# Pair sums of the seven-product chains written back into PSUM, gate products and gated additions on VectorE

## The chip, the core and the metric

The kernel runs on one core of one Trainium2 chip. A core has five engines that matter here: TensorE (PE; its weight loads are shown as PEld), VectorE (DVE), ScalarE (ACT), GpSimd (POOL) and SyncE (SP), which issues the DMAs. Each has its own queue and runs it in order; they wait for each other through semaphores. Matmul results land in PSUM (eight banks), everything else lives in SBUF. The metric is the device time of one execution, in microseconds (us).

## What is computed

One layer of a diffusion backbone for two token groups: 128 context and 512 latent tokens, 640 columns in the kernel, which keeps channels on the partitions. Shapes are D_MODEL = 1024, D_FF = 2816, all float32. The change touches the two SwiGLU feed-forward steps (up and down projection) and the projection of the GLA branch.

```python
def swiglu(h, w_gate, w_up, w_down):
    return (jax.nn.silu(h @ w_gate) * (h @ w_up)) @ w_down

def trunk_layer(x, mod, ...):
    h = modulate(rms_norm(x, norm_ffn1), sh1, sc1)
    x = x + 0.5 * gt1 * swiglu(h, w_ffn1_gate, w_ffn1_up, w_ffn1_down)
    h = modulate(rms_norm(x, norm_mix), sh2, sc2)
    y = mixer(h, ...)      # ends: y = (g_a * branch_a + g_b * (o @ w_proj_gla)) @ w_out
    x = x + gt2 * y
    h = modulate(rms_norm(x, norm_ffn2), sh3, sc3)
    return x + 0.5 * gt3 * swiglu(h, w_ffn2_gate, w_ffn2_up, w_ffn2_down)
```

## The kernel before

**Products.** A float32 matmul is made of three passes on a high and a low part of each operand. `split` (L108, L109) makes them: ScalarE copies the high part, VectorE subtracts it for the low part. Both weights and activations are split in this way.

**Seven products in place of eight.** A job (`Pair7`) is a 2 x 2 block product: two output tiles of 128 rows (i = 0, 1), each of two halves of NH = 320 columns. It is computed by the seven-product scheme. Four sums of weight blocks, S1 to S4 (L492, L494, L496, L498), are made by GpSimd in the raw weight tile, each needed by later splits of that tile. `prep` runs the list STEPS up to a wanted step. For a gate or up job a product is 4 x 3 = 12 matmuls of 128 x 320 (L516), for a down job 9 or 6.

**Strides and banks.** `Pipe.stride` runs one job, with the tail of the job before it (`prev`) and the first weight steps of the job after it (`ahead`) put in between. A job takes three PSUM banks of six that turn: A for products 1, 6, 7 and 4, C for product 2, B for products 5 and 3. TensorE's order in a stride is 1, 2, then 3 of the job before (tail3), 6, 5, then 4 of the job before (tail4), 7.

**Take hooks.** After each product a hook takes what it needs. In the class `Take`, `p1`, `p16` and `p167` copy bank A to SBUF on ScalarE (u, w, u: L605 or L657, L613, L617), because A goes on accumulating; `p2`, `p5` and `p53` add a pair on VectorE (u + C, u + B, w + B); `p1674` takes the finished A. The third product is added onto B, so TensorE waits there until p5 has read B (L620 for a gate job, L664 for others); the seventh is added onto A, so TensorE waits until p16 has copied A (L613).

**The jobs the change touches** use `TakeMul`, where a pair sum does not go out but is put onto a tile `into`: p2, p5 and p53 add in SBUF (L664), and `onto` multiplies on GpSimd (L661) for an up job (`into` is the SiLU of the gate) and for the last projection (`TakeY`, `into` is the branch gate read from DRAM). `TakeDown.onto` (L774) adds gate times sum to the residual stream X on VectorE. After p53 of an up job `Hidden7.first` subtracts the halves of x0 (L707, GpSimd), and place 1 of the next stride splits x0 into high and low; `second` does the same for x1 with three more sums (L719 to L721). The last part of each feed-forward step uses `HiddenPlain`, without sums.

**Order.** Each feed-forward step runs a list of jobs: gate, the four down jobs of the part before, up, then gate, up, gate, up. There are 20 up jobs, 24 down jobs and four `TakeY` jobs in all. In the feed-forward steps `pin` fixes every engine's order to the order in which the code is written; the last projection is not pinned, and there a scheduler places instructions. Weight loads are issued by SyncE when a raw tile comes free.

## Time and profile before

| | |
|---|---|
| median of 3 runs | 1566.56 us (1566.31 to 1567.09) |
| the profiled execution | 1564.67 us, span 1562.9 us |
| TensorE busy | 1481.5 us, 95% of the span |
| VectorE busy | 1175.6 us, 75% |
| ScalarE busy | 785.7 us, 50% |
| GpSimd busy | 582.2 us, 37% |
| waits of TensorE in L516 | 42.2 us |
| granted TensorE clock, mean | 0.989 |

The span is the time from the first to the last instruction; a busy share is an average over stages. In the rows below an instruction is named by its line, engine, operation and tiles (out<-in, buffer numbers left out): wraw is a raw weight tile, wspl a split weight, pb a PSUM bank, g the tiles x0, x1 and `into`, hn and sqh the copies u and w, pg a page of activations.

### The profile page before, as it was taken

Reading aid. Unit: us, or ns where it says so; the run is one execution under the profiler, and the core shown is the slowest. Engines: PE = TensorE matmul, PEld = TensorE weight load, DVE = VectorE, ACT = ScalarE, POOL = GpSimd, SP = SyncE. Lnnn points to the kernel's source line nnn. Section 1 sums busy time; section 2 is a strip of 40 time slices with the busy share of each in tenths; the row PEclk is TensorE's granted clock in tenths of the full one; section 3 lists DMA queues with packets and bytes.
Section 4 is the critical chain, followed back from the end, with each engine's and each line's share of the span. In section 5 each row is a group of like instructions: output and inputs, shape, how many; then the busy total and the mean of one; then the engine's idle time right before and its main releaser. Section 6 shows DMA issues by size and latency. Waiting matters only on the chain.

```text
span 1562.9 us, 27799 instructions
## 1 busy us (share of the span) xinstructions
PE 1481.5 (95%) x10994; PEld 1429.8 (91%) x10994; DVE 1175.6 (75%) x2001; ACT 785.7 (50%) x1687; POOL 582.2 (37%) x470
## 2 busy tenths in 40 slices
PE   7989999999999999999899999999999998998997
PEld 6988889999998999999899998999898998998997
DVE  6759769769768688385866658778777967977976
ACT  5535445445555546454454445346545445544554
POOL 1534655564620000001234314620355565566440
PEclk8999999999999999999999999999999999999999
DMA  9454222222235320222148456354211321321232
GB/s 361 146 211 141 81 68 95 82 68 95 82 102 190 110 68 32 90 65 89 56 172 279 168 182 237 124 192 148 82 55 62 102 82 44 112 71 59 96 103 100
DMA packets 150426, 183.54 MB, mean 117 GB/s; under 512 B 4799, under 2 KB 124983, under 8 KB 150295
## 3 DMA queue, kind: packets, MB, share of 16 engines
q1 hardware_dynamic: 150295, 181.76, 34.8%
q8 instruction: 86, 1.41, 0.4%
q14 instruction: 45, 0.37, 0.1%
HBM read 167.59 MB, written 14.16 MB: 116 GB/s over the span
## 4 chain that ended last, share of the span: by engine, by line
PE 47%; DVE 30%; POOL 10%; ACT 5%; issue 5%; DMA 2%; POOLq 0%; SPq 0%; ACTq 0%; DVEq 0%
PE pb L516 16%; DVE wspl L109 13%; PE pb L139 6%; PE pb L386 5%; PE mm L1040 5%; DVE pg L774 5%; DVE pg L109 4%; POOL g L661 3%; ACT wspl L108 3%; PE mm L139 2%; POOL wraw L496 2%; PE sc L1189 2%; DVE hn L664 2%; POOL wraw L498 2%; PE sm L215 2%
## 5 line engine op out<-in xcount | busy, mean ns | idle before, releaser
L516 PE MATMUL pb<-pg,wspl 128*128 128x320 f32 x5556 | 839.7, 311 | 42.2 <-DVE g L620 15.1
L516 PEld LDWEIGHTS pb<-pg,wspl 128*128 128x128 f32 x5556 | 819.7, 189 | 59.4 <-DVE g L620 19.3
L109 DVE TENSOR_TENSOR wspl<-wraw,wspl 128x512 fp32r<-128x512 f32 (+2 forms) x676 | 513.3, 780 | 197.2 <-ACT wspl L108 195.3
L108 ACT ACTIVATE wspl<-wraw 128x512 fp32r<-128x512 f32 (+2 forms) x676 | 378.8, 588 | 254.2 <-POOL wraw L496 74.5
L496 POOL TENSOR_TENSOR wraw<-wraw 128x512 f32<-128x512 f32 (+2 forms) x74 | 89.8, 1214 | 241.2 <-DVE wspl L109 227.7
L494 POOL TENSOR_TENSOR wraw<-wraw 128x512 f32<-128x512 f32 (+2 forms) x74 | 104.1, 1407 | 102.0 <-DVE wspl L109 102.0
L386 PE MATMUL pb<-pg,wspl 128*128 128x320 f32 (+2 forms) x864 | 132.7, 311 | 1.6 <-DVE wspl L109 1.6
L386 PEld LDWEIGHTS pb<-pg,wspl 128*128 128x128 f32 x864 | 127.2, 188 | 2.1 <-DVE wspl L109 1.9
L498 POOL TENSOR_TENSOR wraw<-wraw 128x512 f32<-128x512 f32 (+2 forms) x74 | 110.0, 1486 | 3.1
L139 PE MATMUL pb<-pg,wspl 128*128 128x320 f32 x672 | 105.2, 315 | 3.0 <-DVE pg L1460 2.7
L139 PEld LDWEIGHTS pb<-pg,wspl 128*128 128x128 f32 x672 | 100.5, 190 | 5.1 <-DVE pg L1460 4.0
L492 POOL TENSOR_TENSOR wraw<-wraw 128x512 f32<-128x512 f32 (+2 forms) x74 | 96.4, 1303 | 4.2
L109 DVE TENSOR_TENSOR pg<-g,pg 128x640 fp32r<-128x640 f32 x86 | 85.1, 1006 | 16.0 <-ACT pg L108 16.0
L108 ACT ACTIVATE pg<-g 128x640 fp32r<-128x640 f32 x86 | 58.4, 682 | 63.8 <-DVE g L679 26.0
L1040 PE MATMUL mm<-wspl,pg 128*128 128x256 f32 x672 | 88.9, 289 | 0.1
L1040 PEld LDWEIGHTS mm<-wspl,pg 128*128 128x128 f32 x672 | 83.9, 195 | 0.5 <-ACT pg L1142 0.3
L1243 POOL TENSOR_TENSOR rs<-ms,negh 128x5 f32<-128x5 f32 x4 | 4.7, 1175 | 208.1 <-DVE ms L1241 208.1
L661 POOL TENSOR_TENSOR g<-g,hn 128x320 f32<-128x320 f32 x48 | 53.2, 1109 | 62.8 <-DVE hn L664 51.3
L109 DVE TENSOR_TENSOR pg<-pg,pg 128x320 fp32r<-128x320 f32 (+2 forms) x84 | 57.3, 729 | 11.9 <-ACT pg L108 11.7
L613 ACT ACTIVATE sqh<-pb 128x320 f32<-128x320 f32 x74 | 31.8, 430 | 54.1 <-PE pb L516 54.1
L617 ACT ACTIVATE hn<-pb 128x320 f32<-128x320 f32 x74 | 31.8, 430 | 41.4 <-PE pb L516 41.4
L131 PE MATMUL pb<-pg,wspl 128*128 128x320 f32 x288 | 48.0, 321 | 3.9 <-DVE pg L366 1.9
(219 smaller groups left out, 1745.6 us busy)
## 6 DMA issues: line engine op xcount, KB each, us to landing
pg<-in_w_ada_dram SPq DMA_DIRECT2D x72, 512.0 KB, 7.0
wraw<-in_w_ffn_gate_dram SPq DMA_DIRECT2D x22, 1024.0 KB, 5.0
wraw<-in_w_ffn_up_dram SPq DMA_DIRECT2D x22, 1024.0 KB, 5.0
wraw<-in_w_ffn_down_dram SPq DMA_DIRECT2D x28, 768.0 KB, 4.4
wraw<-in_w_in_dram SPq DMA_DIRECT2D x22, 512.0 KB, 3.5
wraw<-in_w_in_dram SPq DMA_DIRECT2D x10, 1024.0 KB, 5.5
wraw<-in_w_out_dram SPq DMA_DIRECT2D x8, 1024.0 KB, 5.2
wraw<-in_w_ffn_down_dram SPq DMA_DIRECT2D x12, 512.0 KB, 3.4
```

Of the source, the lines that this page charges most:

```text
L108: S.activation(out=hi, in_=src, func=AF.Copy)
L109: eng.tensor_tensor(out=lo, in0=src, in1=hi.bitcast(F32), op=ALU.subtract)
L139: T.matmul(out=bank(ps, hf)[:, 0:NH], lhsT=w[a][k], rhs=acts[k][:, b, hf * NH:(hf + 1) * NH], start=(k == 0 and ti == 0), stop=(k == nk - ...
L386: T.matmul(out=ps[:, 0:c1 - c0], lhsT=w[a][i], rhs=acts[i][:, b, c0:c1], start=(i == 0 and ti == 0), stop=(i == nk - 1 and ti == 2))
L492: G.tensor_tensor(out=self.a21, in0=self.a21, in1=self.a22, op=ALU.add)
L494: G.tensor_tensor(out=self.a11, in0=self.a22, in1=self.a11, op=ALU.subtract)
L496: G.tensor_tensor(out=self.a11, in0=self.a11, in1=self.a21, op=ALU.subtract)
L498: G.tensor_tensor(out=self.a12, in0=self.a12, in1=self.a11, op=ALU.subtract)
L516: T.matmul(out=bank, lhsT=self.w[i][s][k], rhs=x[k][:, t, :], start=first and k == 0 and ti == 0, stop=k == self.n - 1 and ti == 2, skip_g ...
L661: return G.tensor_tensor(out=x, in0=x, in1=part, op=ALU.mult)
L774: V.scalar_tensor_tensor(out=self.X[k][:, a:b], in0=x[:, o:o + b - a], scalar=self.gate[:, k, r:r + 1], in1=self.X[k][:, a:b], op0=ALU.mul ...
L1040: T.matmul(out=ps_out, lhsT=h2[k][:, a, t * P:(t + 1) * P], rhs=w[b][k], start=(k == 0 and ti == 0), stop=(k == KD - 1 and ti == 2))
```

## The change

The sum of p2, p5 and p53 is written into a PSUM bank instead of SBUF: p2 into C, p5 into C again (`self.free`), p53 into B. The bank is then an operand of what follows. The gate products of `onto` move from GpSimd to VectorE, with one operand in PSUM. The gated addition of the down jobs reads the sum from PSUM. `Hidden7.first` does product and difference on VectorE, the product in PSUM; where it is called without a bank (the first pair of each feed-forward step) the difference moves to VectorE too. In p16 ScalarE's copy of A is now written ahead of the product.

```diff
@@ -652,36 +652,30 @@
     class TakeMul(Take):
 
 
-        def p1(self, ps):
-            self.u = sm_tile([P, NH], "hn")
-            S.activation(out=self.u, in_=ps, func=AF.Copy)
-
-        def onto(self, part, i, hf):
+
+        def p2(self, ps):
+            V.tensor_tensor(out=ps, in0=self.u, in1=ps, op=ALU.add)
+            self.free = ps
+
+        def p16(self, ps):
+            Take.p16(self, ps)
+            self.onto(self.free, 0, 0)
+
+        def onto(self, ps, i, hf):
             x = self.into[i][:, hf * NH:(hf + 1) * NH]
-            return G.tensor_tensor(out=x, in0=x, in1=part, op=ALU.mult)
-
-        def add(self, part, ps):
-            V.tensor_tensor(out=part, in0=part, in1=ps, op=ALU.add)
-
-        def p2(self, ps):
-            self.add(self.u, ps)
-
-        def p16(self, ps):
-            self.onto(self.u, 0, 0)
-            Take.p16(self, ps)
+            V.tensor_tensor(out=x, in0=ps, in1=x, op=ALU.mult)
 
         def p5(self, ps):
-            self.add(self.u, ps)
-            self.mixed = self.onto(self.u, 1, 1)
+            V.tensor_tensor(out=self.free, in0=self.u, in1=ps, op=ALU.add)
+            self.onto(self.free, 1, 1)
 
         def p1674(self, ps):
-            x = self.into[1][:, 0:NH]
-            V.tensor_tensor(out=x, in0=ps, in1=x, op=ALU.mult)
+            self.onto(ps, 1, 0)
             self.done(1)
 
         def p53(self, ps):
-            self.add(self.w, ps)
-            self.last = self.onto(self.w, 0, 1)
+            V.tensor_tensor(out=ps, in0=self.w, in1=ps, op=ALU.add)
+            self.onto(ps, 0, 1)
             self.done(0)
 
     class Hidden7:
@@ -697,14 +691,19 @@
             split(h[:, 0, :], h[:, 1, :], x)
             return h
 
-        def first(self, x0):
+        def first(self, x0, ps=None):
             def work():
                 h = self.put(x0)
                 self.b11.append(even(h))
                 self.t1.append(odd(h))
 
             self.x0 = x0
-            G.tensor_tensor(out=x0[:, NH:N], in0=x0[:, NH:N], in1=x0[:, 0:NH], op=ALU.subtract)
+            right = x0[:, NH:N]
+            if ps is None:
+                V.tensor_tensor(out=right, in0=right, in1=x0[:, 0:NH], op=ALU.subtract)
+            else:
+                V.tensor_tensor(out=ps, in0=ps, in1=right, op=ALU.mult)
+                V.tensor_tensor(out=right, in0=ps, in1=x0[:, 0:NH], op=ALU.subtract)
             pipe.at(1, work)
 
         def second(self, x1):
@@ -746,7 +745,8 @@
 
             pipe.at(place, work)
 
-        def first(self, x):
+        def first(self, x, ps):
+            V.tensor_tensor(out=x[:, NH:N], in0=ps, in1=x[:, NH:N], op=ALU.mult)
             self.put(x, 1)
 
         def second(self, x):
@@ -760,22 +760,23 @@
             self.into = self.g.x0, self.g.x1
             TakeMul.p1(self, ps)
 
+        def p53(self, ps):
+            V.tensor_tensor(out=ps, in0=self.w, in1=ps, op=ALU.add)
+            self.hid.first(self.into[0], ps)
+
         def done(self, i):
-            (self.hid.second if i else self.hid.first)(self.into[i])
+            self.hid.second(self.into[i])
 
     class TakeDown(TakeMul):
         def __init__(self, mp, gate, X):
             self.mp, self.gate, self.X = mp, gate, X
 
-        def onto(self, x, i, hf):
+        def onto(self, ps, i, hf):
             k = 2 * self.mp + i
             for r, a, b in HSEG[hf]:
                 o = a - hf * NH
-                V.scalar_tensor_tensor(out=self.X[k][:, a:b], in0=x[:, o:o + b - a], scalar=self.gate[:, k, r:r + 1],
+                V.scalar_tensor_tensor(out=self.X[k][:, a:b], in0=ps[:, o:o + b - a], scalar=self.gate[:, k, r:r + 1],
                                        in1=self.X[k][:, a:b], op0=ALU.mult, op1=ALU.add)
-
-        def p1674(self, ps):
-            self.onto(ps, 1, 0)
 
         def done(self, i):
             pass
```

How the order moves is shown at three places. The first two are the same stretch of the first feed-forward step: the end of the up job of f = 10 (blocks 10 and 11 of D_FF; its `into` tiles are g_2594 and g_2595) and the gate job of f = 12 behind it (raw weights wraw_3065), while the weights of the next up job (wraw_3179) are prepared. GpSimd's queue before, from S2 of the gate job (L494):

```order
L494 TENSOR_TENSOR wraw_3065<-wraw_3065 128x4x128
L661 TENSOR_TENSOR g_2595<-g_2595,hn_3258 128x320
L498 TENSOR_TENSOR wraw_3065<-wraw_3065 128x4x128
L661 TENSOR_TENSOR g_2594<-g_2594,sqh_3213 128x320
L707 TENSOR_TENSOR g_2594<-g_2594 128x320
L496 TENSOR_TENSOR wraw_3179<-wraw_3179 128x4x128
L492 TENSOR_TENSOR wraw_3179<-wraw_3179 128x4x128
L494 TENSOR_TENSOR wraw_3179<-wraw_3179 128x4x128
```

and with the change:

```order
L494 TENSOR_TENSOR wraw_3065<-wraw_3065 128x4x128
L498 TENSOR_TENSOR wraw_3065<-wraw_3065 128x4x128
L496 TENSOR_TENSOR wraw_3179<-wraw_3179 128x4x128
L492 TENSOR_TENSOR wraw_3179<-wraw_3179 128x4x128
L494 TENSOR_TENSOR wraw_3179<-wraw_3179 128x4x128
L720 TENSOR_TENSOR g_2594<-g_2595,g_2594 128x320
L498 TENSOR_TENSOR wraw_3179<-wraw_3179 128x4x128
```

The three instructions of `onto` and `first` are gone; S4 (L498) follows S2 at once, and S3 of the next job (L496) follows S4; L720 there is L721 before. VectorE's queue over the same stretch, from p5's sum to p1674; before:

```order
L664 TENSOR_TENSOR hn_3258<-hn_3258,pb_3219 128x320
L109 TENSOR_TENSOR wspl_3262<-wraw_3065,wspl_3262 128x512
L109 TENSOR_TENSOR wspl_3282<-wraw_3065,wspl_3282 128x512
L609 TENSOR_TENSOR g_3297<-hn_3280,pb_3267 128x320
L109 TENSOR_TENSOR wspl_3300<-wraw_3065,wspl_3300 128x512
L109 TENSOR_TENSOR wspl_3305<-wraw_3179,wspl_3305 128x512
L664 TENSOR_TENSOR sqh_3213<-sqh_3213,pb_3219 128x320
L109 TENSOR_TENSOR wspl_3323<-wraw_3179,wspl_3323 128x512
L109 TENSOR_TENSOR wspl_3341<-wraw_3179,wspl_3341 128x512
L109 TENSOR_TENSOR pg_3359<-g_2594,pg_3359 128x640
L679 TENSOR_TENSOR g_2595<-pb_3144,g_2595 128x320
```

and with the change, from p5's sum on:

```order
L669 TENSOR_TENSOR pb_3145<-hn_3258,pb_3219 128x320
L666 TENSOR_TENSOR g_2595<-pb_3145,g_2595 128x320
L109 TENSOR_TENSOR wspl_3262<-wraw_3065,wspl_3262 128x512
L109 TENSOR_TENSOR wspl_3282<-wraw_3065,wspl_3282 128x512
L609 TENSOR_TENSOR g_3297<-hn_3280,pb_3267 128x320
L109 TENSOR_TENSOR wspl_3300<-wraw_3065,wspl_3300 128x512
L109 TENSOR_TENSOR wspl_3305<-wraw_3179,wspl_3305 128x512
L764 TENSOR_TENSOR pb_3219<-sqh_3212,pb_3219 128x320
L705 TENSOR_TENSOR pb_3219<-pb_3219,g_2594 128x320
L706 TENSOR_TENSOR g_2594<-pb_3219,g_2594 128x320
L109 TENSOR_TENSOR wspl_3323<-wraw_3179,wspl_3323 128x512
L109 TENSOR_TENSOR wspl_3341<-wraw_3179,wspl_3341 128x512
```

Behind p5's sum stands its product (L666), and behind p53's sum (L764) product and difference (L705, L706), ahead of the weight split that followed the sum before. The third place is the last projection, where the scheduler orders VectorE's work: the first strides' p2 and p53 (g_10668 and g_10790 are the `into` tiles of the first and the second job). VectorE before:

```order
L664 TENSOR_TENSOR hn_10796<-hn_10796,pb_10777 128x320
L109 TENSOR_TENSOR wspl_10836<-wraw_10711,wspl_10836 128x512
L664 TENSOR_TENSOR sqh_10733<-sqh_10733,pb_10739 128x320
L109 TENSOR_TENSOR wspl_10855<-wraw_10711,wspl_10855 128x512
L1488 TENSOR_TENSOR g_10668<-g_10668,pg_10255 128x640
L109 TENSOR_TENSOR pg_10670<-g_10668,pg_10670 128x640
```

and with the change:

```order
L657 TENSOR_TENSOR pb_10777<-hn_10796,pb_10777 128x320
L666 TENSOR_TENSOR g_10790<-pb_10777,g_10790 128x320
L109 TENSOR_TENSOR wspl_10836<-wraw_10711,wspl_10836 128x512
L677 TENSOR_TENSOR pb_10739<-sqh_10732,pb_10739 128x320
L666 TENSOR_TENSOR g_10668<-pb_10739,g_10668 128x320
L109 TENSOR_TENSOR wspl_10855<-wraw_10711,wspl_10855 128x512
L1489 TENSOR_TENSOR g_10668<-g_10668,pg_10255 128x640
L109 TENSOR_TENSOR wspl_10889<-wraw_10711,wspl_10889 128x512
L109 TENSOR_TENSOR pg_10670<-g_10668,pg_10670 128x640
```

The product of p16 of the second job (g_10790) stands right behind its p2, the product of p53 of the first (L666 onto g_10668) between p53's sum and the addition L1489, which is L1488 before.

## Rows read from the trace of the kernel before

**Rows 1.** The page, parts 1 and 4: busy us (share) xinstructions; the chain's shares.

```profile
PE 1481.5 (95%) x10994; PEld 1429.8 (91%) x10994; DVE 1175.6 (75%) x2001; ACT 785.7 (50%) x1687; POOL 582.2 (37%) x470
...
PE 47%; DVE 30%; POOL 10%; ACT 5%; issue 5%; DMA 2%; POOLq 0%; SPq 0%; ACTq 0%; DVEq 0%
```

**Rows 2.** Waits of TensorE: us in total, times, longest us.

```profile
PE pb L516 <- DVE g L620: 15.1, 15, 3.5
PE pb L516 <- ACT sqh L613: 12.4, 14, 1.2
PE pb L516 <- DVE hn L664: 6.7, 5, 2.8
PE pb L516 <- DVE pg L109: 6.0, 11, 0.9
```

**Rows 3.** Windows: stretch, us, then busy us (x) of PE, PEld, DVE, ACT, POOL.

```profile
298.00:326.10 28.10, 25.37 (x169) 24.64 (x168) 20.69 (x28) 13.82 (x29) 17.38 (x13) 1.00 0.24 76
...
361.50:418.00 56.50, 56.50 (x385) 56.50 (x386) 51.60 (x81) 29.80 (x61) 31.71 (x26) 1.00 0.30 98
```

**Rows 4.** Timeline of the pair: start us, us, instruction xcount [idle before <-releaser].

```profile
283.98 1.27 POOL L661 TENSOR_TENSOR g<-g,hn 128x320 f32<-128x320 f32 x1 [1.03 <-DVE hn L664]
...
285.20 1.75 POOL L498 TENSOR_TENSOR wraw<-wraw 128x512 f32<-128x512 f32 x1
...
288.86 0.48 DVE L664 TENSOR_TENSOR sqh<-sqh,pb 128x320 f32<-128x320 f32 x1
...
290.76 0.88 POOL L707 TENSOR_TENSOR g<-g 128x320 f32<-128x320 f32 x1
291.60 1.30 POOL L496 TENSOR_TENSOR wraw<-wraw 128x512 f32<-128x512 f32 x1
292.93 0.63 ACT L108 ACTIVATE wspl<-wraw 128x512 fp32r<-128x512 f32 x1 [3.21 <-POOL wraw L496]
...
298.11 0.48 DVE L620 TENSOR_TENSOR g<-hn,pb 128x320 f32<-128x320 f32 x1
...
298.64 7.47 PE L516 MATMUL pb<-pg,wspl 128*128 128x320 f32 x48 [0.60 <-DVE g L620]
...
305.16 0.48 DVE L642 TENSOR_TENSOR g<-sqh,pb 128x320 f32<-128x320 f32 x1
...
306.84 0.42 ACT L613 ACTIVATE sqh<-pb 128x320 f32<-128x320 f32 x1
...
307.31 12.87 PE L516 MATMUL pb<-pg,wspl 128*128 128x320 f32 x86 [1.20 <-ACT sqh L613]
...
326.71 7.46 PE L516 MATMUL pb<-pg,wspl 128*128 128x320 f32 x48 [1.54 <-DVE g L620]
```

**Rows 5.** Groups by line: busy us, mean ns | idle; L720 by itself: ns min/median/max.

```profile
L661 POOL TENSOR_TENSOR g<-g,hn 128x320 f32<-128x320 f32 x48 | 53.2, 1109 | 62.8 <-DVE hn L664 51.3 <-ACT g L643 10.4 <-issue 1.1
...
L707 POOL TENSOR_TENSOR g<-g 128x320 f32<-128x320 f32 x17 | 15.5, 910 | 1.2
...
L664 DVE TENSOR_TENSOR sqh<-sqh,pb 128x320 f32<-128x320 f32 x48 | 22.9, 478 | 2.8 <-PE pb L516 2.8
...
L720 DVE TENSOR_TENSOR g<-g x17: 491/492/1054, 102.4 to 1441.8; 128x320 f32<-128x320 f32 x17
...
L774 DVE SCALAR_TENSOR_TENSOR pg<-sqh,hg,pg 128x128 f32<-128x128 f32 x24 | 26.9, 1120 | 0.0
...
L393 DVE SCALAR_TENSOR_TENSOR pg<-pb,hg,pg 128x128 f32<-128x128 f32 x24 | 7.6, 344 | 1.8 <-PE pb L386 1.8
```

**Rows 6.** Last projection and second feed-forward step: timeline; a window, PEclk third last.

```profile
999.86 1.91 DVE L1488 TENSOR_TENSOR g<-g,pg 128x640 f32<-128x640 f32 x1 [1.61 <-POOL g L661]
...
1023.53 10.54 PE L516 MATMUL pb<-pg,wspl 128*128 128x320 f32 x60 [2.79 <-DVE hn L664]
...
1174.45 7.78 PE L516 MATMUL pb<-pg,wspl 128*128 128x320 f32 x33 [3.54 <-DVE g L620]
...
1174.50:1180.40 5.90, 5.90 (x22) 5.90 (x23) 5.87 (x9) 2.87 (x5) 2.80 (x2) 0.50 0.00 0
```

## The prediction, made before the change was run

> **What bounds the kernel now.** The page first: TensorE is busy for 95% of the span and VectorE for 75%, and the chain that ended last runs 47% through TensorE, 30% through VectorE and 10% through GpSimd [rows 1]. So a change that takes no matmul away can only give back what TensorE idles, and the next view is TensorE's waits. In the seven-product chains (L516) four waits carry nearly all of it: 15.1 us for L620, 12.4 for L613, 6.7 for L664 and 6.0 for the hidden splits of L109 [rows 2]. All four are evictions or splits on VectorE or ScalarE, yet the engine behind them is not full. In the stretch of four down jobs TensorE does 385 matmuls in 56.50 us without a stall (0.147 us each); in a pair of one up and one gate job it is busy for 25.37 of 28.10 us and VectorE for 20.69 [rows 3]. A pair is 2 x 7 x 12 = 168 matmuls, 24.7 us at that pace. From the first third-product restart to the next one (298.64 to 326.71, 28.07 us) 3.4 us are lost, 1.20 + 1.54 of them as the two gaps shown [rows 4]. The other 0.65 is the restart: 0.3 us for each stall.
>
> The timeline of one such pair says why [rows 4]. At 283.98 GpSimd multiplies the p5 half of the up job (L661); step S4 of the weights (L498) stands behind it and starts at 285.20, and the weight splits that wait for S4 hold VectorE until p53's sum at 288.86. Then GpSimd multiplies again, subtracts (L707, 290.76) and only then does S3 of the next job (L496, 291.60). ScalarE, which needs S3 for the next weight split, sat idle for 3.21 us, until 292.93. From there the delay runs through VectorE to L620 at 298.11: the pair sum of the gate job, which reads bank B before TensorE may add its third product there. TensorE waits 0.60 us, in the next pair 1.54. From L620 to L642 VectorE has work in its queue without a pause of note; L642 at 305.16 lets ScalarE do its SiLU and then L613 (306.84), and TensorE's seventh product waits 1.20 us for that.
>
> **The change part by part.** *Taken from GpSimd:* the 72 gate products of L661 (three in each of 24 jobs: the 48 of the row and 24 like them) at 1.11 us and the 17 differences of L707 at 0.91 [rows 5]: 95 us of GpSimd. What counts is not the sum but the places: S4 no longer stands behind a product that waits for p5, nor S3 behind two that wait for p53.
>
> *Given to VectorE:* 89 instructions of 320 columns with one operand in PSUM. The sum of this kind from PSUM takes 0.478 us [rows 5]: 42.5 us in all, 1.9 us for an up job that feeds a Hidden7 (15 of them), 1.4 for the other nine jobs, and two differences by themselves. Writing the sum into PSUM stands in no row. Not below 0.48, since the same columns go through; the upper bound is the slowest 320-column row of two operands, 1.05 [rows 5]. I take 0.48: reading PSUM made these sums no slower than the best case of two SBUF operands (0.49).
>
> *Made cheaper on VectorE:* the gated additions of the 24 down jobs now read PSUM. From SBUF the 128-column piece took 1.12 us, from PSUM in another stage 0.34 [rows 5]: 0.78 for that piece alone, so some 19 us over 24 jobs, and the 192-column piece beside it gains too. This lies in stretches where TensorE does not wait [rows 3]; I count nothing for it. If that cover went, it would only be a gain.
>
> *In the pair*, hand-walked on the trace's clock. TensorE stops at 298.64 - 0.60 = 298.04, after the second product of the next up job. Counted back by 0.147 us a matmul the gate job began at 282.2, the third product in its stride ended at 287.5, its sixth at 289.2, its fourth (in the tail) at 292.8, its seventh at 294.5. S4 can start some 2 us sooner, so VectorE is free at 287.5 and p53's three instructions end at about 289, where L707 ended at 291.6. S3 is done long before; the next weight split follows L613 at about 289.7, not 292.93. Then the hidden split, the fourth product's eviction (292.8), the second split and the copy of the seventh product (294.6) bring L620 to about 295.7 to 296.2, against 298.04, when TensorE needs it: a margin near 2 us in place of a stall of 0.6 or 1.5. L642 follows L620 by 7.05 us and L613 follows by 1.68 more [rows 4]; by the earlier L620 L613 starts at 304.4 and ends at 304.9. The seventh product is due at 298.04 + 48 x 0.147 = 305.1. That margin is thin, and the up job now has one more VectorE product (0.48) ahead of the seventh weights' split, and another behind p5. What is queued behind these: the split's low half, and on GpSimd S2, which waits for it; GpSimd's own product no longer stands ahead of S1, which pays for that. So I count the L620 waits as gone and half of the L613 waits.
>
> *The banks:* C is now held to p5 and B through the product. Six banks turn, three for each job, so C's bank is wanted again two jobs later, some 10 us after its last reader. This costs nothing; the cover is the rotation, and with it gone TensorE would wait for p5 once a job. The orders of TensorE and of the DMA queue are as before; ScalarE's differs only in the last projection.
>
> *The last projection.* There x0's addition (L1488) waits 1.61 us for GpSimd and then runs 1.91 us beside GpSimd's S2 [rows 6]. The products are now on VectorE ahead of it. It starts some 2 us sooner, and the waits for L664 of this stage, the longest of them 2.79 us, come from its lateness, by way of the hidden split and p5 behind it on VectorE. That stall and the one of 3.54 us in the second FFN were each followed by slow matmuls, in the second case at a granted clock of 0.50, the lower level of 1.2 GHz: 60 matmuls took 10.54 us and 33 took 7.78, where 0.147 each gives 8.8 and 4.9 [rows 6]. Without the 0.2 us that a last matmul runs on, 4.3 us go with the two stalls.
>
> *The sum:* L620 15.1 + 15 x 0.3 = 19.6; L613, half, 6.2 + 7 x 0.3 = 8.3; L664, four fifths, 5.4 + 4 x 0.3 = 6.6; hidden splits, two thirds (the first down job's t2 split has little slack), 4.0 + 7 x 0.3 = 6.1; clock 4.3. Together 44.9 us. The profiled execution took 1564.67 us, 1.8 of them outside its span of 1562.9, and the median of the runs is 1.9 above it: 1564.7 - 44.9 + 1.9 = **1521.7 us**. The ceiling is all four waits: 40.2 + 45 x 0.3 + 4.3 = 58 us, 1508.6.
>
> **The rivals.** *A: only the first stall goes.* L642 and L613 stand in VectorE's and ScalarE's own queues, and the new products there eat what is gained. For it: 7 us of VectorE work between L620 and L642. Against it: that work starts from L620, which comes sooner. Then only L620 and its clock loss (2.7) go: 22.3 us, 1544.3.
>
> *B: slower, VectorE becomes the bound in the pairs.* The up job's four added instructions make 20.69 + 1.9 = 22.6 us of VectorE in a pair that TensorE needs 24.7 for. It turns once the four instructions of a pair that write PSUM cost 0.5 us more, over 1.0 each, which is the far end above. If then every added instruction lies on the path, 42.5 us: 1609. Against it: no row from PSUM is anywhere near 1.0. The Trainium skill has a rule that points this way (Perfetto Trace Analysis, Optimizing Scalar/DVE Operations): with VectorE saturated, work may be handed to GpSimd; this change does the reverse. By that rule the price would be the same 42.5 us, but its condition, a saturated VectorE, is not what the pairs show.
>
> *C: no change.* The steps S1 to S4, still 1.3 to 1.75 us each, collide with VectorE's splits wherever they now fall, and the sooner start is used up before L620: 1566.6. Against it: ScalarE's 3.21 us of idle time ends with S3, which has nothing left to stand behind.
>
> **How the numbers follow.** The forecast 0.69 (by itself 1508 to 1533), A 0.20, B 0.06, C 0.05. The range runs from the ceiling past A: 1508 to 1547. Faster by over 0.2%, about what a measurement of this kernel can tell from no change: 0.89; within it 0.05; slower 0.06.
>
> **What would show it.** Right: L620 gone from TensorE's waits or under 2 us, L613 between 3 and 8, S3 starting within 0.5 us of its weights, a pair period near 25 us, no lower clock in the last projection and the second FFN, VectorE's total within 15 us of 1176. Wrong: PSUM-written sums well over 0.5 us; VectorE without idle time in the pairs; waits of the same size under other names, above all for a weight split that waits for GpSimd's S2.

## The result, and the profile after

The changed kernel takes **1515.36 us** (median of 4 runs, 1514.91 to 1516.08); the kernel before, in 4 runs beside it, 1566.43 us (1564.15 to 1567.09). The ratio is 0.9677, 95% interval 0.966 to 0.9694: 51 us less. The profiled execution took 1515.8 us, its span is 1514.0.

The page of the changed kernel, parts 1 and 4, answers to [rows 1]:

```profile
PE 1466.2 (97%) x10994; PEld 1424.7 (94%) x10994; DVE 1160.6 (77%) x2090; ACT 783.5 (52%) x1687; POOL 492.1 (33%) x381
...
PE 76%; DVE 13%; issue 3%; ACT 3%; DMA 3%; SPq 1%; POOL 1%; ACTq 0%; POOLq 0%; DVEq 0%
```

VectorE has 89 instructions more and yet 15.0 us less of busy time; GpSimd has 90 us less. TensorE's share of the last chain went from 47 to 76%.

TensorE's waits in the seven-product chains of the changed kernel (us in total, times, longest us), against [rows 2]:

```profile
PE pb L516 <- ACT sqh L613: 2.8, 7, 1.2
...
PE pb L516 <- DVE pb L669: 1.8, 4, 0.7
...
PE pb L516 <- DVE g L620: 1.5, 1, 1.5
...
PE pb L516 <- DVE wspl L109: 0.4, 1, 0.4
```

L669 is p5's sum, L664 before. The waits of L516 went from 42.2 to 6.4 us. The pair of [rows 4], up f = 10 and gate f = 12, looks like this in the timeline of the changed kernel (start us, us, instruction xcount [idle before <-releaser]):

```profile
264.82 35.36 PE L516 MATMUL pb<-pg,wspl 128*128 128x320 f32 x240
...
274.70 0.49 DVE L764 TENSOR_TENSOR pb<-sqh,pb 128x320 f32<-128x320 f32 x1
274.71 1.29 POOL L496 TENSOR_TENSOR wraw<-wraw 128x512 f32<-128x512 f32 x1 [4.75 <-DVE wspl L109]
275.23 0.50 DVE L705 TENSOR_TENSOR pb<-pb,g 128x320 f32<-128x320 f32 x1
275.76 0.49 DVE L706 TENSOR_TENSOR g<-pb,g 128x320 f32<-128x320 f32 x1
...
282.62 0.48 DVE L620 TENSOR_TENSOR g<-hn,pb 128x320 f32<-128x320 f32 x1
...
289.68 0.47 DVE L642 TENSOR_TENSOR g<-sqh,pb 128x320 f32<-128x320 f32 x1
...
291.36 0.42 ACT L613 ACTIVATE sqh<-pb 128x320 f32<-128x320 f32 x1
```

S3 (L496) starts with p53's sum (L764), when the split that reads its weights has ended (at 274.64), and not 2.74 us after that sum, as in [rows 4]. TensorE runs the 240 matmuls of the 35 us shown without a break. Its order is that of before, so the two matmuls that had to wait can be found again by their place: they start at 285.06 and 292.10. L620 ends at 283.10, 1.96 us ahead of the first; L613 ends at 291.78, 0.32 us ahead of the second.

Three stretches of seven-product chains hold all of the gain: from the first to the last L516 matmul of each, the first feed-forward step took 368.1 us before and 346.1 after, the last projection 58.1 and 53.5, the second feed-forward step 376.6 and 353.2. That is 50.0 us. The first of them begins between 86.6 and 91.0 us in the profiled runs of this study, in all variants, so stretches are compared below beside whole times. Each is of one profiled execution. The feed-forward steps repeat to 0.4 us where an edit leaves them alone (e3_last); the last projection took 57.1 or 58.1 us with its jobs unchanged, for a reason that comes with e1_down:

| kernel | first step | last projection | second step | median, us |
|---|---|---|---|---|
| before | 368.1 | 58.1 | 376.6 | 1566.4 |
| changed | 346.1 | 53.5 | 353.2 | 1515.4 |
| e1_down: down jobs alone | 365.4 | 57.1 | 373.6 | 1559.3 |
| e2_up: up jobs alone | 347.1 | 58.1 | 352.7 | 1522.1 |
| e3_last: last projection alone | 368.1 | 53.3 | 376.2 | 1560.8 |
| e4_sbuf: sums in SBUF | 350.6 | 57.1 | 354.8 | 1526.8 |
| e5_p53: p16, p5 back on GpSimd | 351.2 | 53.0 | 357.9 | 1526.8 |
| e6_p5: p53 back on GpSimd | 355.4 | 53.0 | 363.6 | 1536.2 |
| e7_blind: GpSimd busy, no waits | 348.6 | 53.2 | 355.5 | 1525.9 |
| e8_wait: GpSimd busy and waiting | 376.1 | 57.2 | 388.4 | 1584.5 |
| e9_dve: 82 more on VectorE | 347.3 | 54.3 | 353.6 | 1520.7 |
| e10_third: last difference on VectorE | 343.9 | 53.8 | 350.4 | 1510.3 |
| e11_order: GpSimd's order alone | 358.8 | 57.1 | 364.2 | 1543.3 |
| e12_third_late: last difference behind S4 | 345.3 | 53.0 | 351.3 | 1512.0 |

### The profile page after: what moved, and what is told of

Its sections match the earlier page's. It is cut to its first block, busy times and chain, and to the rows that moved or that the text cites. A ratio compares the mean times of both kernels' runs of the same rounds, so it can differ in the third digit from the quotient of the medians.

```text
span 1514.0 us, 27844 instructions
## 1 busy us (share of the span) xinstructions
PE 1466.2 (97%) x10994; PEld 1424.7 (94%) x10994; DVE 1160.6 (77%) x2090; ACT 783.5 (52%) x1687; POOL 492.1 (33%) x381
## 4 chain that ended last, share of the span: by engine, by line
PE 76%; DVE 13%; issue 3%; ACT 3%; DMA 3%; SPq 1%; POOL 1%; ACTq 0%; POOLq 0%; DVEq 0%
PE pb L516 45%; PE pb L139 6%; PE pb L386 5%; PE mm L1041 5%; DVE wspl L109 4%; PE mm L139 2%; PE sc L1190 2%; DVE pg L109 2%; PE sm L215 2%; PE sm L1041 2%; PE pb L131 1%; ACT wspl L108 1%; DVE pg L366 1%; DMA pg<-in_w_ada_dram 1%; PE sm L1222 1%
## 5 line engine op out<-in xcount | busy, mean ns | idle before, releaser
L516 PE MATMUL pb<-pg,wspl 128*128 128x320 f32 x5556 | 824.3, 310 | 6.4 <-ACT sqh L613 2.8
L516 PEld LDWEIGHTS pb<-pg,wspl 128*128 128x128 f32 x5556 | 815.2, 188 | 12.6 <-ACT sqh L613 4.6
L109 DVE TENSOR_TENSOR wspl<-wraw,wspl 128x512 fp32r<-128x512 f32 (+2 forms) x676 | 502.2, 762 | 132.8 <-ACT wspl L108 130.3
L496 POOL TENSOR_TENSOR wraw<-wraw 128x512 f32<-128x512 f32 (+2 forms) x74 | 89.8, 1213 | 331.0 <-DVE wspl L109 317.5
L494 POOL TENSOR_TENSOR wraw<-wraw 128x512 f32<-128x512 f32 (+2 forms) x74 | 108.6, 1467 | 96.2 <-DVE wspl L109 96.2
L139 PE MATMUL pb<-pg,wspl 128*128 128x320 f32 x672 | 105.2, 315 | 2.9 <-DVE pg L1461 2.7
L498 POOL TENSOR_TENSOR wraw<-wraw 128x512 f32<-128x512 f32 (+2 forms) x74 | 103.1, 1394 | 4.3
L109 DVE TENSOR_TENSOR pg<-g,pg 128x640 fp32r<-128x640 f32 x86 | 82.6, 977 | 13.5 <-ACT pg L108 13.1
L613 ACT ACTIVATE sqh<-pb 128x320 f32<-128x320 f32 x74 | 32.1, 434 | 88.1 <-PE pb L516 88.0
L778 DVE SCALAR_TENSOR_TENSOR pg<-pb,hg,pg 128x320 f32<-128x320 f32 (+1 forms) x144 | 58.6, 435 | 12.6 <-PE pb L516 10.8
L109 DVE TENSOR_TENSOR pg<-pg,pg 128x320 fp32r<-128x320 f32 (+2 forms) x84 | 55.8, 712 | 13.1 <-ACT pg L108 13.1
L617 ACT ACTIVATE hn<-pb 128x320 f32<-128x320 f32 x74 | 32.2, 435 | 57.0 <-PE pb L516 56.6
L605 ACT ACTIVATE hn<-pb 128x320 f32<-128x320 f32 x74 | 32.0, 433 | 55.3 <-PE pb L516 40.8
```

The source lines that it names most:

```text
L109: eng.tensor_tensor(out=lo, in0=src, in1=hi.bitcast(F32), op=ALU.subtract)
L139: T.matmul(out=bank(ps, hf)[:, 0:NH], lhsT=w[a][k], rhs=acts[k][:, b, hf * NH:(hf + 1) * NH], start=(k == 0 and ti == 0), stop=(k == nk - ...
L494: G.tensor_tensor(out=self.a11, in0=self.a22, in1=self.a11, op=ALU.subtract)
L496: G.tensor_tensor(out=self.a11, in0=self.a11, in1=self.a21, op=ALU.subtract)
L498: G.tensor_tensor(out=self.a12, in0=self.a12, in1=self.a11, op=ALU.subtract)
L516: T.matmul(out=bank, lhsT=self.w[i][s][k], rhs=x[k][:, t, :], start=first and k == 0 and ti == 0, stop=k == self.n - 1 and ti == 2, skip_g ...
```

## The experiments

**Which jobs carry it.** The change was taken apart by kind of job; the old `TakeMul` stays beside the new one under the name `OldMul`.

e1_down:

```diff
-    class TakeUp(TakeMul):
+    class TakeUp(OldMul):
...
-    class TakeY(TakeMul):
+    class TakeY(OldMul):
```

> The kernel before, with the change in its 24 down jobs alone: their pair sums are written into PSUM and the gated additions read PSUM; up jobs and the last projection keep their products and first differences on GpSimd. Theory T (the gain is GpSimd's queue: the steps S3 and S4 of the weights no longer stand behind a product that waits for VectorE): GpSimd's rows are the same ones in the same order, so the gain is 0 to 6 us, 1560 to 1567 us, and the waits for g L620 (15.1 us), sqh L613 (12.4) and pg L109 (6.0) stay within a third of what they were. Rival R (the gain is VectorE's own time: fewer long reads of SBUF beside GpSimd): the down jobs are where the 128-column additions fell from 1.12 to 0.34 us, so over half of the 51 us comes with them, 1540 us or less.

Measured: 1559.28 us, ratio 0.9958 (0.9943 to 0.9973). This is 1 us below T's range, and far from R. VectorE lost 31.6 us of busy time (1144.0 where it had 1175.6), but the waits stayed:

```profile
PE pb L516 <- DVE g L620: 13.0, 12, 3.5
PE pb L516 <- ACT sqh L613: 12.4, 14, 1.2
PE pb L516 <- DVE pg L109: 6.0, 11, 0.9
```

So VectorE's total was not what bound the kernel. Most of the few us come from the pairs next to the down jobs: three of the fifteen L620 waits are gone. One us of the seven does not come from the change. The last projection, whose jobs are the old ones here, still has its stall of 2.79 us for p5's sum, but the granted clock behind it (third last) is 1.00, where it was 0.50 for 3.4 us in the kernel before:

```profile
1020.60:1031.00 10.40, 10.37 (x70) 10.37 (x71) 8.79 (x13) 4.83 (x9) 3.76 (x3) 1.00 0.53 162
```

The same stall was followed by the full clock in e11_order too. A stall of this length brings the lower clock in some executions and not in others.

e2_up, the mirror image:

```diff
-    class TakeDown(TakeMul):
+    class TakeDown(OldMul):
...
-    class TakeY(TakeMul):
+    class TakeY(OldMul):
```

> The kernel before, with the change in its 20 up jobs alone (sums into PSUM, products and first difference on VectorE); down jobs and the last projection as before. Theory T: both FFN stretches give what they gave in the full change, 22.0 and 23.4 us, so 1521 us, between 1517 and 1527. Rival R (VectorE's time in the down jobs): 1540 us or more, since the up jobs only add work to VectorE.

Measured: 1522.07 us, ratio 0.9719 (0.970 to 0.9738), as T has it. The up jobs carry 44 of the 51 us, though here VectorE is busy for 1191.5 us, 16 more than before.

e3_last has `OldMul` in the up and the down jobs.

> The kernel before, with the change in its four last-projection jobs alone; up and down jobs as before. Theory T: that stretch of seven-product chains took 58.1 us before and 53.5 after, and the slow matmuls behind its 2.8 us stall go with it: 1560 to 1563 us, and no wait over 1 us in it. Rival N (the last projection's stall had another cause, in the splits of the hidden operand): 1565 to 1567 us, stretch within 1 us of 58.1.

Measured: 1560.8 us, ratio 0.9961 (0.9945 to 0.9977), the stretch 53.3 us, its longest wait 0.7 us, as theory T has it. Taken alone the three kinds give 7, 44 and 6 us, in sum 57 and not 51: the down jobs' 7 is nearly all shared with the up jobs, whose waits it shortens. With the up jobs changed, the two feed-forward steps gain only 0.5 us more from the down jobs (699.8 us in e2_up, 699.3 in the full change).

**Occupied, or waiting?** Two kernels put 89 GpSimd operations back where the old ones stood; they write a scratch tile that nobody reads. All other engines keep the order of the changed kernel.

e7_blind:

```diff
+    def dummy(x):
+        G.tensor_tensor(out=sm_tile([P, KD * 32], "junk").rearrange("p (k c) -> p k c", k=KD), in0=cs, in1=cs, op=ALU.mult)
...
             Take.p16(self, ps)
             self.onto(self.free, 0, 0)
+            self.extra(0, 0)
...
+        def extra(self, i, hf):
+            dummy(self.into[i][:, hf * NH:(hf + 1) * NH])
```

and likewise behind p5 and p53; two stand behind the first difference (junk and cs have 256 columns).

> The changed kernel, with a GpSimd operation of 256 columns put in each place where a product or first difference stood on GpSimd before; it reads a constant and writes a scratch tile, so it waits for nothing and nobody waits for it. GpSimd's time is back (some 85 to 95 us), its waits for VectorE are not. Theory T as far as it says that the wait in front of S3 and S4 is what cost the time: at most 1520 us, with at most 3 us of waits for g L620 and sqh L613 over the changed kernel's. Rival O (it was GpSimd's occupied time, about 1.1 us ahead of each S3 and S4): 1530 to 1550 us, with the waits back to at least a third of 15.1 and 12.4 us.

e8_wait differs in one operand:

```diff
-        G.tensor_tensor(out=sm_tile([P, KD * 32], "junk").rearrange("p (k c) -> p k c", k=KD), in0=cs, in1=cs, op=ALU.mult)
+        G.tensor_tensor(out=sm_tile([P, KD * 32], "junk").rearrange("p (k c) -> p k c", k=KD), in0=x[:, 0:KD * 32].rearrange("p (k c) -> p k c", k=KD), in1=cs, op=ALU.mult)
```

> As the run before it, but the added GpSimd operation reads the product that VectorE has just formed, so it waits for VectorE where the old product waited; its result goes to a scratch tile that nobody reads. VectorE, ScalarE and TensorE run what the changed kernel runs. Theory T: the queue is blocked as before, and somewhat longer, since the wait ends one VectorE product (0.5 us) later: 1550 to 1580 us, with the waits for g L620 and sqh L613 back. Rival L (the gain is the shorter way of x0 and x1 through VectorE, not the steps behind it): at most 1525 us, since no consumer of x0 or x1 waits for the added operations. Rival O: the same as the run before it.

Measured: e7_blind 1525.88 us, ratio 0.9744 (0.9724 to 0.9765); e8_wait 1584.45 us, ratio 1.0118 (1.0103 to 1.0133). The groups of GpSimd of the two (busy us, mean ns | idle before, and what ended it), e7_blind's first:

```profile
L688 POOL TENSOR_TENSOR junk<-cs 128x256 f32<-128x256 f32 x89 | 81.6, 928 | 0.7 <-DVE mod L222 0.5
```

```profile
L688 POOL TENSOR_TENSOR junk<-g,cs 128x256 f32<-128x256 f32 x89 | 87.6, 992 | 186.3 <-DVE g L667 92.0 <-DVE g L715 55.3 <-DVE g L712 18.7
```

The same operations, in the same places but for the twelve named next, cost 10 us where they wait for nothing, and 69 us where they wait for VectorE. Of e7_blind's 10 us, 4.8 lie in the feed-forward steps. Another 5.4 lie ahead of the last projection: nothing held its twelve operations in place there, they went ahead of the sums of the projection's operand, and TensorE waited for those. That is why T's bound of 1520 was missed; its other half held (L620 0.8 us and L613 1.3 us over the changed kernel). Rival O, which asked for 1530 us or more, is out by its time. Its sign in the waits is not wholly absent: L613 has twelve waits and 4.1 us, a third of what it had before, so the occupied time does use up the thin margin in five of eight pairs.

e8_wait ended above the kernel before and 4 us above T's range. Its waits for L620 are 22.6 us (15.1 before) and those for L613 7.0 (12.4 before); where TensorE is over 2 us late by L620 already, L613 is no longer waited for. The pair shows how they come about (timeline of GpSimd and L620):

```profile
295.54 0.49 DVE L715 TENSOR_TENSOR g<-pb,g 128x320 f32<-128x320 f32 x1
296.11 1.81 POOL L688 TENSOR_TENSOR junk<-g,cs 128x256 f32<-128x256 f32 x2 [3.69 <-DVE g L715]
297.89 1.30 POOL L496 TENSOR_TENSOR wraw<-wraw 128x512 f32<-128x512 f32 x1
299.22 0.63 ACT L108 ACTIVATE wspl<-wraw 128x512 fp32r<-128x512 f32 x1 [3.27 <-POOL wraw L496]
...
304.40 0.48 DVE L620 TENSOR_TENSOR g<-hn,pb 128x320 f32<-128x320 f32 x1
```

S3 stands behind two operations, the first of which waited 3.69 us, ScalarE idles 3.27 us for S3 (3.21 in [rows 4]), and L620 is late. x0 and x1 are made by VectorE's short products as in the changed kernel, and none of their readers in the feed-forward steps waited for an added operation, so rival L falls as the whole cause. That it came out slower than the kernel before fits the place of the added operations: both wait for the difference, two VectorE operations behind p53's sum and not the one that the expectation reckoned with, and S3 starts 3.40 us after that sum, against 2.74. The cause is the wait at the head of an in-order queue.

**GpSimd's order alone.** e11_order leaves every product on GpSimd and only issues S4 ahead of p5's product, and S3 ahead of p53's product and the difference. No other engine's order changes.

```diff
             ahead("S3")
+            if self.prev:
+                self.prev.take.late(0)
...
             ahead("S4")
+            j.take.late(1)
...
     class TakeUp(TakeMul):
+        def p5(self, ps):
+            self.add(self.u, ps)
+
+        def p53(self, ps):
+            self.add(self.w, ps)
+
+        def late(self, i):
+            if i:
+                self.onto(self.u, 1, 1)
+            else:
+                self.onto(self.w, 0, 1)
+                self.done(0)
```

> The kernel before with one thing changed, the order of GpSimd's queue in the two feed-forward steps: in the up jobs S4 is issued ahead of p5's product and S3 ahead of p53's product and the first difference. All products stay on GpSimd, with SBUF sums; every other engine and the DMA queue run the same instructions in the same order. Theory T in its strongest form (the place in the queue alone): the waits for g L620, sqh L613 and the hidden splits go as in the changed kernel, at GpSimd's full occupation, which cost 2.5 us in each feed-forward step as measured with operations that wait for nothing, and without the 7 us of the down jobs: 1525 to 1540 us. Rival S (VectorE's shorter products are needed too, since x0 and x1 now come later still, behind S3 and S4): 1545 to 1566 us. Rival Q (the queue's order is nothing): 1564 to 1568 us, or slower.

Measured: 1543.25 us, ratio 0.9863 (0.9841 to 0.9885), between T's range and that of S. In the two feed-forward steps, the only ones that it touches, it gives 21.7 of the changed kernel's 45.4 us: nearly half of the gain needs no faster engine at all. What it leaves (L628 is L620, L621 is L613, L672 is L664, L715 is L707):

```profile
PE pb L516 <- ACT sqh L621: 10.6, 14, 1.2
PE pb L516 <- DVE hn L672: 6.7, 5, 2.8
PE pb L516 <- DVE pg L109: 4.2, 7, 0.9
PE pb L516 <- DVE g L628: 4.2, 3, 3.5
...
ACT pg L108 <- POOL g L715: 27.5, 15, 1.9
```

The L620 waits are gone but for three, and the L613 waits are all there. This is the outcome of rival A of the prediction (1544.3 us), though not by its reason, since no product was added to VectorE here. The last row says what is missing: S3 and S4 are on time, but ScalarE now waits up to 1.9 us for GpSimd's difference before it can split x0, once in each of 15 up jobs. So what rival S says holds for the rest. The two waits of TensorE hang together: in the changed kernel L613 ends 8.68 us after L620 ends (283.10 to 291.78), while the matmuls that wait for them are 7.04 us apart. L620 must be 1.64 us early for L613 to be just in time. Here, in the pair, it was 0.9 us early, and L613 0.6 late; in the next pair it was level, and L613 cost 1.2.

**Which half of the products.** e5_p53 puts p16's and p5's products of the up jobs back on GpSimd, e6_p5 p53's product and the first difference.

```diff
-    class TakeUp(TakeMul):
+    class TakeUp(OldMul):
...
         def p53(self, ps):
             V.tensor_tensor(out=ps, in0=self.w, in1=ps, op=ALU.add)
             self.hid.first(self.into[0], ps)
```

> The changed kernel, with the products after p16 and p5 of the up jobs back on GpSimd (their sums in SBUF); p53's product and the first difference stay on VectorE. So S4 stands behind a product that waits for p5 again, S3 behind nothing. Theory T as the prediction walked it: p53's sum starts as late as before (VectorE held by the splits after S4), but its product and difference take 1.0 us and not 2.4, and S3 is early: the L620 waits mostly go, those for L613 and the hidden splits come back in part: 1520 to 1540 us. Rival Z (the two blocks add, each with the share of its instructions): of the 45 us in the two FFN stretches 20 to 25 are lost, 1535 to 1541 us. Rival K (S4 carries all): 1550 us or more.

```diff
     class TakeUp(TakeMul):
         def p53(self, ps):
-            V.tensor_tensor(out=ps, in0=self.w, in1=ps, op=ALU.add)
-            self.hid.first(self.into[0], ps)
+            V.tensor_tensor(out=self.w, in0=self.w, in1=ps, op=ALU.add)
+            x = self.into[0][:, NH:N]
+            G.tensor_tensor(out=x, in0=x, in1=self.w, op=ALU.mult)
+            self.hid.first(self.into[0])
```

> The changed kernel, with p53's product and the first difference of the up jobs back on GpSimd (p53's sum in SBUF); the products after p16 and p5 stay on VectorE. So S3 stands behind two operations that wait for p53, S4 behind nothing. Theory T as the prediction walked it: S3 starts 2 us later than in the changed kernel, but p53's sum comes 1.3 us sooner than before the change: the margin of some 2 us at L620 is nearly used up, most L620 waits stay away, 1520 to 1540 us. Rival Z (the two blocks add): 1535 to 1541 us. Rival K3 (S3 carries all): 1550 us or more.

Measured: e5_p53 1526.76 us, ratio 0.9741 (0.9725 to 0.9757), L620 waits 1.5 us and L613 8.9; e6_p5 1536.18 us, ratio 0.9799 (0.9777 to 0.9821), L620 3.7 and L613 11.2. Both lie in T's range, e6_p5 in that of Z as well. The losses against the changed kernel are 11 and 21 us, in sum 32, well under the 44 that the up jobs carry. Either half by itself clears most L620 waits, both together are needed for the 1.64 us that L613 asks: L620 is early by 0.5 to 0.6 us in five of the eight pairs that gain in the changed kernel and by 1.96 in three with e5_p53, by 0.6 in four and by nothing in four with e6_p5. p53's block in front of S3 is the heavier.

**What PSUM has to do with it.** e4_sbuf keeps all products on VectorE and writes the sums into SBUF again.

```diff
         def p2(self, ps):
-            V.tensor_tensor(out=ps, in0=self.u, in1=ps, op=ALU.add)
-            self.free = ps
+            V.tensor_tensor(out=self.u, in0=self.u, in1=ps, op=ALU.add)
+            self.free = self.u
```

(p5 and p53 likewise; p16's copy of A is written behind the product again, which leaves the order of ScalarE and of GpSimd as in the changed kernel)

> The changed kernel, with the pair sums of up, down and last-projection jobs written into SBUF as before the change, so that all products and gated additions on VectorE read SBUF; GpSimd's queue is that of the changed kernel. Theory T (GpSimd's queue carries the gain): VectorE gets dearer where GpSimd works beside it, by the 7 us that the down jobs gave by themselves and up to half as much again in the up jobs: 1520 to 1530 us. Rival M (VectorE can take the products only because they read and write PSUM): products near 1.0 us each, over half of the gain lost, 1541 us or more.

Measured: 1526.77 us, ratio 0.9742 (0.9726 to 0.9758): theory T, and 11 us of the 51 hang on PSUM. In the feed-forward steps the parts line up: the order of GpSimd's queue alone gives 21.7 us (e11_order), the products on VectorE 17.6 more (e4_sbuf), the sums in PSUM the last 6.1. The groups of VectorE by form, first of e4_sbuf, then of the changed kernel:

```profile
L666 DVE TENSOR_TENSOR g<-hn,g 128x320 f32<-128x320 f32 x48 | 35.3, 735 | 1.7 <-ACT g L643 0.8
...
L706 DVE TENSOR_TENSOR g<-sqh,g 128x320 f32<-128x320 f32 x15 | 20.2, 1343 | 0.5
L705 DVE TENSOR_TENSOR sqh<-sqh,g 128x320 f32<-128x320 f32 x15 | 17.0, 1135 | 0.5
```

```profile
L666 DVE TENSOR_TENSOR g<-pb,g 128x320 f32<-128x320 f32 x76 | 37.0, 487 | 13.2 <-PE pb L516 11.2 <-ACT g L643 0.8
...
L669 DVE TENSOR_TENSOR pb<-hn,pb 128x320 f32<-128x320 f32 x48 | 23.5, 489 | 11.1 <-ACT hn L617 10.5
...
L705 DVE TENSOR_TENSOR pb<-pb,g 128x320 f32<-128x320 f32 x15 | 7.5, 500 | 0.5
L706 DVE TENSOR_TENSOR g<-pb,g 128x320 f32<-128x320 f32 x15 | 7.4, 492 | 0.5
```

**How much more VectorE bears.** e9_dve adds 82 operations of the kind that writes PSUM, one behind each of 52 products:

```diff
             V.tensor_tensor(out=x, in0=ps, in1=x, op=ALU.mult)
+            if (i, hf) != (1, 0):
+                V.tensor_tensor(out=ps, in0=ps, in1=x, op=ALU.max)
```

and two behind each of the 15 differences of `Hidden7.first`.

> The changed kernel, with 82 more VectorE operations: behind each product that the change gave to VectorE (p16, p5, p53 of up jobs that feed a Hidden7 and of the last projection, and the first difference) a further operation of 320 columns that reads the sum's PSUM bank and writes it again, after its last use. VectorE's time grows by some 40 us (82 x 0.49). Rival B of the prediction (VectorE is the bound in the pairs, every added operation lies on the path): 1545 to 1556 us. Theory T with a margin near 2 us at L620 in a pair and 2.0 us added there: at most half of it is seen, 1515 to 1535 us.

Measured: 1520.73 us, ratio 0.9708 (0.9687 to 0.973). 82 operations of 0.49 to 0.50 us, 40 us in all, cost 5 us, 2.4 of them in the three stretches. Rival B falls: VectorE's busy time in the pairs is not the bound. The 2.0 us added to a pair move L620 by nothing in four of the eight pairs and by 0.4 us in the others. (VectorE's total grew by 24.8 us only; the weight splits of 512 columns got 9 us cheaper, 795 ns each where the changed kernel has 811.)

**The same idea once more.** One GpSimd operation that waits for VectorE is left between p5 and S4: x0's second difference (L720, 1132.76 to 1133.88 in the first pair of the second step, after a wait of 2.76 us). e10_third gives it to VectorE, e12_third_late issues it behind S4.

```diff
-                G.tensor_tensor(out=x0[:, 0:NH], in0=x1[:, NH:N], in1=x0[:, 0:NH], op=ALU.subtract)
+                V.tensor_tensor(out=x0[:, 0:NH], in0=x1[:, NH:N], in1=x0[:, 0:NH], op=ALU.subtract)
```

> The changed kernel, with the last GpSimd operation on the hidden operand (x0's second difference, 17 of 1.12 us, which waits for VectorE between p5 and S4) on VectorE too, so that GpSimd's queue in the feed-forward steps holds the steps S1 to S4 alone. Theory T: what is left of waits in the seven-product chains is 6.4 us, half of it at the start of the second feed-forward step behind S4; 1511 to 1515 us. Rival B (17 more VectorE operations of 0.49 us cost more than that): 1516 to 1520 us.

```diff
+            def last():
                 G.tensor_tensor(out=x0[:, 0:NH], in0=x1[:, NH:N], in1=x0[:, 0:NH], op=ALU.subtract)
...
             ahead("S4")
+            self.do(8)
```

> The changed kernel, with the same GpSimd operation (x0's second difference) left on GpSimd but issued behind S4 instead of ahead of it; all other engines run the same order. Theory T: S4 no longer waits for VectorE's difference, the third weights and hidden splits after it come sooner, but the third hidden split waits longer: 1511 to 1517 us. Rival (it was not in the way): 1514 to 1517 us with the same 6.4 us of waits.

Measured: e10_third 1510.33 us, ratio 0.9652 (0.963 to 0.9675); e12_third_late 1511.97 us, ratio 0.9658 (0.9637 to 0.9679). e10_third is 0.7 us below T's range, and its rival B falls; e12_third_late lies in T's range, with 4.9 us of waits where its rival said 6.4. They are the fastest kernels here. The intervals overlap that of the changed kernel, so by the times alone 5 and 3 us are not certain; the stretches give 5.0 and 2.7 us less in the two feed-forward steps, and the waits of e10_third shrink to two entries:

```profile
PE pb L516 <- DVE pb L669: 2.4, 3, 1.4
...
PE pb L516 <- DVE g L620: 1.4, 1, 1.4
```

In e10_third the way from L620 to L613 is shorter too: L613 ends 7.29 us after L620 in the pairs, where it was 8.68, and its margin grows from 0.32 to 1.32 us.

## Why the prediction was right

Forecast 1521.7, measured 1515.4: inside the range, 6 us low in the gain. Point by point:

- **The cause** holds as it was told: S3 and S4 behind products that wait for VectorE. e8_wait brings the loss back by the wait alone, e11_order takes half of it away by the order alone, e7_blind shows that the occupied time is minor. The prediction said "what counts is not the sum but the places"; the places carry it, but not all: in the feed-forward steps e11_order left 23.7 us, in which x0 waits for GpSimd's slower products, and those needed the shorter way through VectorE as well.
- **The walk through the pair** came out to a few tenths. L620: a margin near 2 us, measured 1.96. L642 7.05 us behind L620, measured 7.06; L613 1.68 behind that, measured 1.68. L613's margin 0.2, measured 0.32. One step was off without harm: S4 starts not some 2 but 3.95 us sooner (268.27; 281.25 on before's clock by TensorE's place, against 285.20). VectorE is free no sooner than the walk says (274.64, which is 287.62), because ScalarE's copy of the gate job's first product (L605, 271.23) stands ahead of the splits that follow S4.
- **The step that was mis-sized** is what was made of that last number. The walk said that L613 fits, and the sum then left half of its waits standing because the margin was thin. That half had no row behind it. A margin that repeats in every pair of the same order is there or it is not: in eight pairs it is 0.31 to 0.33 us, and all eight waits of 1.2 us are gone. Of the 2.8 us left, 1.2 are in the first pair of the second step, the rest are six waits in the first down job of a part, 0.41 to 0.48 us before and now 0.22 to 0.28. With 0.3 us for each wait that went, L613 gave 9.6 + 7 x 0.3 = 11.7 us against 8.3. The hidden splits of L109 went entirely, 6.0 + 11 x 0.3 = 9.3 against 6.1. L620 left one wait of 1.5 us, so 13.6 + 14 x 0.3 = 17.8 against 19.6; L664 gave 4.9 + 0.3 = 5.2 against 6.6. The clock's 4.3 came to some 4.0: the 60 matmuls of the last projection take 9.07 us where they took 10.54, the 33 behind the other stall 2.5 us less. This is 48.0 us. Two small waits that the sum left out (weight splits of L109, 0.8 us before and 0.4 after; L617, 0.8 and none) make it 49.8, and the three stretches give 50.0. The profiled executions differ by 1564.67 - 1515.8 = 48.9, since 1.1 us are lost outside the stretches. So the terms and the restart of about 0.3 us hold, in one profiled execution of each kernel. The other 2 us of the medians' 51 are the 1.9 us that were added for before's profiled run lying below its median; after's lies 0.4 above.
- **The lower clock** is gone where it was expected to be. In the window of the changed kernel that answers to the last of [rows 6], right behind the stall of 1.45 us that is left there, the granted clock (third last) is 1.00 and not 0.50, and 39 matmuls run where 22 did. For the last projection this was in part the luck of the execution, as e1_down shows. The rows are the last projection's 60 matmuls and the window:

```profile
999.11 9.07 PE L516 MATMUL pb<-pg,wspl 128*128 128x320 f32 x60 [0.65 <-DVE pb L669]
...
1146.50:1152.40 5.90, 5.90 (x39) 5.73 (x40) 5.87 (x9) 2.89 (x5) 2.79 (x2) 1.00 0.01 3
```

- **VectorE's price**: 0.48 us taken, 0.487 to 0.500 measured for the forms that read and write PSUM. Its total was to come within 15 us of 1176; it is 1160.6, just past that edge, and below where the added products should have put it. The down jobs' additions alone take 31.6 us off (e1_down), where the rows gave 19 for one of their pieces, and the weight splits of 512 columns, which have less GpSimd work beside them, fell from 847 to 811 ns, 17 us in all. The down jobs' additions, counted at nothing, are worth 0.5 us in the steps when the up jobs are changed too, and 7 alone.
- **The last projection**: x0's addition (L1489, L1488 before) takes 0.82 us and waits for nobody, where the row read 1.91 and a wait of 1.61. The stretch gave 4.6 us.
- **The signs.** L620 is under 2 us (1.5), the pair's period near 25 (24.64, from 285.06 to 309.70), S3 starts 0.07 us after the split that reads its weights, and the lower clock is gone. Two signs were missed narrowly, L613 (2.8, where 3 to 8 was asked) and VectorE's total. The banks cost nothing: no wait of TensorE ends with a product that reads C or B.
- **The rivals.** A did not happen to the full change. Its outcome, L613 still waiting when L620 no longer does, came with the halves of the change, by what the prediction held against it: L613 follows L642 and so L620. B is refused by e9_dve. The Trainium skill's rule named there (Perfetto Trace Analysis, Optimizing Scalar/DVE Operations) has a second half, that GpSimd and VectorE share a read port, so moving work between them may not help. No run here has a saturated VectorE, so its first half stays untried. Of the second half the price is seen in e4_sbuf, where the products moved to VectorE take 0.735 us with two SBUF operands and 0.487 with one; but the move helps there all the same, by 40 us. C is refused by L620, which is 1.96 us early: the sooner start of S3 is not used up on the way.

## What to carry to other kernels

On an engine that runs its queue in order, an operation that waits for another engine costs whatever stands behind it, not its own length: look for the cheap step that others need early, and see what it is queued behind. Before work is moved to another engine, try whether a different order on the same engine gives part of the gain, and count both. When two waits hang on one chain, work out how early the first must be for the second to vanish; clearing only the first looks like half a success and is the same lateness read a second time.

## What the runs showed of the hardware

- VectorE writes a PSUM bank that it reads in the same instruction at hardly more than it takes to write SBUF: 0.489 to 0.500 us for 320 columns, against 0.478 for the sums before. In e9_dve the 52 operations behind products lie between 485 and 500 ns, the 23 with GpSimd at work beside them like the others.
- With both operands in SBUF the same products ran at 0.735 us in the mean, and the two of `Hidden7.first`, beside GpSimd's weight steps, at 1.135 and 1.343 (e4_sbuf). The mean hides two kinds: of 48 products the 28 with GpSimd idle took 477 to 494 ns, the 20 with GpSimd at work beside them 1.09 us in the mean. The products of the changed kernel, with one operand in PSUM, took 488 ns beside GpSimd and 485 without (L666). The Trainium skill has this (SBUF — State Buffer, Who interferes with whom): a VectorE instruction with two SBUF inputs contends with GpSimd's reads, one with at most one SBUF input, outside the two-port modes, does not. The traces agree. Last, the row of the 48 products (ns, min/median/max):

```profile
L666 DVE TENSOR_TENSOR g<-hn,g x48: 477/492/1590, 95.9 to 1480.0; 128x320 f32<-128x320 f32 x48
```

- Seventeen operations more on VectorE made VectorE's total smaller: e10_third adds 8.2 us and ends at 1150.4 us, 10.2 under the changed kernel. The splits of 640 columns of the hidden operand, which had run beside GpSimd's difference, fell from 1.100 to 0.931 us.
